# A second expert layer with its table stationary: sums that come out with model dimensions on partitions

## The chip, the cores and the metric

One core of a Trainium2 chip runs the whole program. The metric is the device time of one execution in microseconds. Of the core's engines, TensorE (PE) multiplies matrices, with a stationary operand that is loaded ahead and a moving one of up to 512 columns that streams past it; VectorE (DVE) and ScalarE (ACT) do elementwise work; SyncE (SP) issues transfers.

## The reference

Two blocks over 256 tokens of 1024 model dimensions. Each ends with an expert layer (`peer`) of 16384 experts of one neuron each, 8 heads, 16 chosen per head; the second block's layer does the same with its own weights and shared keys. The rest of both blocks (attention and recurrences, cross attention) stands ahead of these layers.

```python
def peer(xn, w_pq, subkeys, peer_u, peer_v):
    ...                                # scores, top 16 of each half, top 16 of the sums
    gate = jax.nn.softmax(best_s, axis=-1).astype(xn.dtype)
    ...
        act = jax.nn.gelu(jnp.einsum('thkd,td->thk', peer_u[eb], xb), approximate=False) * gb
        return jnp.einsum('thk,thkd->td', act, peer_v[eb])
...
        x = x + peer(rmsnorm(x, g_peer[l]), w_pq[l], peer_subkeys[l], peer_u[l], peer_v[l])
    return rmsnorm(x, g_final)
```

The second block takes the first one's normalized x, begins with a norm of its own, and its result is normalized with `final_g_2`.

## The kernel before

x lies transposed: eight blocks `X[k]` of 128 model dimensions on partitions, 256 tokens along them. An expert layer is computed densely: all 16384 experts are applied to all tokens, with gates that are zero where an expert was not chosen. The 16384 experts are 128 tables of 128 experts; a table of the first layer (`u`) and one of the second (`v`) have 128 x 1024 numbers.

Every table comes by DMA as `raw` (four buffers) and is split by `weight` (L282 to L290) in two halves of 512 columns, each into a high part `wh` (ACT, L274) and the rest `wl` (DVE, L275), seven buffers a half of each. A product is three matmuls: high by high, high by rest, rest by high (L298 for the first layer, tile `ph`: per table 24 matmuls, eight blocks of the table stationary, 256 tokens moving).

The gated activations come from `prep` (L1210): `hid` is multiplied with the gates `gt` (DVE, L1218), which `fetch` (L1208) has SP load from `gd` in memory, and is split into `dah` (ACT, L274) and `dal` (DVE, L275), four tables in one call. The loop at the end of `peer` takes the 128 `v` tables in order; for each it issues the matmuls of the second layer (L1274), then the next piece of a `u` table as long as there are any (`ug`; `AHEAD` is 47, so that 94 of the 128 `u` tables are done ahead of the loop and the other 34 lie between the first `v` tables), then the next step of `prep` for the four tables behind. With the `u` tables gone, `v` tables follow each other, and `prep` runs as far ahead of them as buffers let it.

The second layer has the activations stationary (128 tokens a time) and the table moving, 512 columns: 12 matmuls for a table, into four PSUM banks `acc[th][dh]`, tokens on partitions (`th` a half of the tokens, `dh` of the dimensions). The last two tables are taken bank by bank, so that banks are complete one after another. `tokens` (L1252) adds x by 16 matmuls with the identity, in the second half of the loop.

Between the peers, `between` (L1286) copies the four banks to `xt`, transposes them by 16 matmuls (`pot`, L1306), copies the result into x (L1310, L1312), feeds the next norm's split input `xnh` (ACT, L408) and `xnl` (DVE, L411), on which the next projections `mm` start, and makes the statistics of both norms from `xt`: four Squares 1024 wide with sums along the free side (L1318, L1321), a product with `gfin` (L1319), an rsqrt by small DVE steps, and `spread` (L371), which brings the factors to the layout of x. At the end `finish` (L1341) reads the banks directly: four Squares, products with `gfin` (L1351), the rsqrt, the scaling and the store.

The order of each engine's instructions is that of the code, with the streams interleaved by a scheduler at build time; each engine runs its own in that order and waits at semaphores.

Of the kernel before, what the change touches and what calls it, by code (L numbers as in the profile page):

```python
# [233 lines left out]
class Net:  # L234
# [679 lines left out]
    def patterns(self):  # L914

        nc = self.nc
        self.iota2 = self.sm("iota2", 256, F16).rearrange("p (i t) -> p i t", t=2)
        nc.vector.tensor_copy(self.iota2, self.c("iota").unsqueeze(2).broadcast_to([128, 128, 2]))
        self.iota16, self.runs16 = (self.sm(n, 256, BF16).rearrange("p (a r) -> p a r", a=16)
                                    for n in ("iota16", "runs16"))  # L920
        for y, x in ((self.iota16, self.c("iota", 16)), (self.runs16, self.c("runs"))):
            nc.vector.tensor_copy(y, x.unsqueeze(2).broadcast_to([128, 16, 16]))
# [68 lines left out]
    def peer(self, N, g, wpq, sub, shared, u, v, gelu, final):  # L991

# [251 lines left out]
        acc = [[self.ac("acc") for _ in range(2)] for _ in range(2)]  # L1244
        gf = None

        def tokens():

            nc.sync.dma_start(gf, final)
            for th in range(2):  # L1250
                for k in range(8):
                    nc.tensor.matmul(acc[th][k // 4][:, k % 4 * 128:k % 4 * 128 + 128],  # L1252
                                     self.X[k][:, 128 * th:128 * th + 128], self.c("ident"), start=False, stop=False)
                    if k % 4 == 3:
                        yield

        xg = tokens()
        for i0 in range(0, 128, 4):
            pn = prep(i0 + 4) if i0 < 124 else iter(())
            ah, al = ops[i0]  # L1260
            w = {}
            for i in range(4):
                w[i] = self.weight(v[i0 + i])

                todo = [(i, q % 2, q // 2) for q in range(4)]
                if i0 + i == 126:
                    todo = []
                elif i0 + i == 127:
                    todo = [(2 + q % 2, q // 4, q // 2 % 2) for q in range(8)]
                for n, th, dh in todo:  # L1270
                    wh, wl = w[n]
                    sl = slice(th * 128, th * 128 + 128)
                    for j, (l, r) in enumerate(((ah, wh), (ah, wl), (al, wh))):
# [5 lines left out]
                if i0 >= 64:  # L1279
                    if gf is None:  # L1280
                        gf = self.big("gfin")
                    next(xg, None)
            drain(pn)
        return acc, gf

    def between(self, acc, gf):  # L1286
# [3 lines left out]
        gg = self.sm("gg", 8)  # L1290
        tt(gg, self.s("g_final"), self.s("norm1_g_2"), ALU.mult)
        xt = []
        for th in range(2):
            xt.append(self.big(f"xt{th}"))
            for dh in range(2):
                sl = slice(512 * dh, 512 * dh + 512)
                if dh:
                    nc.scalar.activation(xt[th][:, sl], acc[th][dh], AF.Copy)
                else:
                    nc.vector.tensor_copy(xt[th][:, sl], acc[th][dh])  # L1300
        for cp in range(4):
            pt = self.mm("pot")
            for a in range(2):
                for th in range(2):
                    c = cp * 2 + a
                    nc.tensor.transpose(pt[:, a * 256 + th * 128:a * 256 + th * 128 + 128],  # L1306
                                        xt[th][:, c * 128:c * 128 + 128], self.c("ident"))
            d = self.x[:, 2 * cp:2 * cp + 2, :].rearrange("p a t -> p (a t)")
            if cp % 2:
                nc.vector.tensor_copy(d, pt)  # L1310
            else:
                nc.scalar.activation(d, pt, AF.Copy)  # L1312
        N = self.norm(self.X, gg, "xn", stats=False)

        v, r = self.sm("bv4", 4), self.sm("br4", 4)
        for th in range(2):
            y = self.big("bty")
            nc.scalar.activation(y, xt[th], AF.Square, accum_out=v[:, th:th + 1])  # L1318
            tt(xt[th], xt[th], gf, ALU.mult)  # L1319
            y = self.big("bty")  # L1320
            nc.scalar.activation(y, xt[th], AF.Square, accum_out=v[:, 2 + th:3 + th])  # L1321
        ts(v, v, 1.0 / D, None, ALU.mult)
# [18 lines left out]
    def finish(self, acc, gf):  # L1341
        nc = self.nc
        tt, ts = nc.vector.tensor_tensor, nc.vector.tensor_scalar
        for th in range(2):
# [166 lines left out]
    def run(self):  # L1511
        tc, nc, I = self.tc, self.nc, self.I
        from contextlib import ExitStack
        with ExitStack() as es:
# [18 lines left out]
            final = [I["gfin"][i:i + 1, :].broadcast_to([128, 1024]) for i in range(2)]  # L1533
            N = self.between(*self.peer(N, self.s("g_peer"), I["w_pq"], I["sub1"], False, I["u1"], I["v1"], AF.Gelu,
                                        final[0]))
            N = self.mixer2(N)
            self.finish(*self.peer(N, self.s("norm2_g_2"), I["w2_pq"], I["sub2"], True, I["u2"], I["v2"],
                                   AF.Gelu_apprx_tanh, final[1]))
# [38 lines left out]
```

## Time and profile before

| | us |
|---|---|
| median of 3 runs (2197.25 to 2197.65) | 2197.36 |
| the profiled execution | 2197.23 |
| its span | 2195.4 |
| PE busy | 2173.8 (99%) |
| weight loads on PE, beside its matmuls | 1979.0 (90%) |
| DVE busy | 1627.1 (74%) |
| ACT busy | 1217.0 (55%) |
| DMA, mean over the span | 201 GB/s |

The span runs from the first instruction to the last; 1.8 us of the execution lie outside it. A matmul's duration in a row includes its way through the array, so neighbours overlap; the distance of two starts is what one costs in a row of them. A chain of waits is read from the last instruction back, at each step to what released it.

### The profile page before, as it was taken

Reading aid. Unit: us, or ns where it says so; the run is one execution under the profiler, and the core shown is the slowest. Engines: PE = TensorE matmul, PEld = TensorE weight load, DVE = VectorE, ACT = ScalarE, POOL = GpSimd, SP = SyncE. Lnnn points to the kernel's source line nnn. Section 1 sums busy time; section 2 is a strip of 40 time slices with the busy share of each in tenths; the row PEclk is TensorE's granted clock in tenths of the full one; section 3 lists DMA queues with packets and bytes.
Section 4 is the critical chain, followed back from the end, with each engine's and each line's share of the span. In section 5 each row is a group of like instructions: output and inputs, shape, how many; then the busy total and the mean of one; then the engine's idle time right before and its main releaser. Section 6 shows DMA issues by size and latency. Waiting matters only on the chain.

```text
span 2195.4 us, 40524 instructions
## 1 busy us (share of the span) xinstructions
PE 2173.8 (99%) x15268; PEld 1979.0 (90%) x15268; DVE 1627.1 (74%) x3504; ACT 1217.0 (55%) x2237; POOL 1.8 (0%) x12
## 2 busy tenths in 40 slices
PE   8999999999999999999999999999999999999998
PEld 8899799999999999888887799999999999887886
DVE  8786676999998665687446567898999655688544
ACT  6463455655666555655445545655666655565443
POOL 0000000000000000000000000000000000000000
PEclk9999999999999999999999999999999999999999
DMA  6442355465677776797555445556577866687653
GB/s 230 141 154 89 118 159 173 146 204 181 212 277 263 238 226 207 236 293 247 186 188 185 147 129 185 161 183 196 196 262 266 262 208 212 220 289 243 214 188 125
DMA packets 178679, 441.12 MB, mean 201 GB/s; under 512 B 13602, under 2 KB 79266, under 8 KB 178484
## 3 DMA queue, kind: packets, MB, share of 16 engines
q1 hardware_dynamic: 177764, 437.11, 61.2%
q8 instruction: 119, 1.95, 0.4%
q10 hardware_dynamic: 720, 1.44, 0.2%
q14 instruction: 76, 0.62, 0.1%
HBM read 403.89 MB, written 34.60 MB: 200 GB/s over the span
## 4 chain that ended last, share of the span: by engine, by line
PE 93%; DVE 4%; DMA 1%; ACT 1%; issue 1%; SPq 0%; ACTq 0%; DVEq 0%
PE ph L298 33%; PE acc L1274 30%; PE mm L298 18%; PE mm L339 3%; PE pg L1164 3%; DVE wl L275 1%; DMA gt<-gd 1%; PE psc L1027 1%; DVE dal L275 0%; PE px L665 0%; ACT wh L274 0%; PE pp L673 0%; DVE hid L1218 0%; PE cs L937 0%; PE pt L679 0%
## 5 line engine op out<-in xcount | busy, mean ns | idle before, releaser
L274 ACT ACTIVATE wh<-raw 128x512 fp32r<-128x512 f32 x1388 | 864.4, 630 | 820.5 <-PE ph L298 272.8
L275 DVE TENSOR_TENSOR wl<-raw,wh 128x512 fp32r<-128x512 f32 x1388 | 941.8, 687 | 437.3 <-ACT wh L274 433.1
L298 PE MATMUL ph<-pxh,wh 128*128 128x256 f32 x2048 | 578.8, 283 | 0.0
L298 PE MATMUL ph<-pxh,wl 128*128 128x256 f32 x2048 | 572.1, 279 | 0.0
L298 PE MATMUL ph<-pxl,wh 128*128 128x256 f32 x2048 | 571.2, 279 | 0.0
L1274 PE MATMUL acc<-wl,dah 128*128 128x512 f32 x1024 | 405.6, 396 | 0.9 <-DVE wl L275 0.4
L1274 PE MATMUL acc<-wh,dah 128*128 128x512 f32 x1024 | 405.5, 396 | 0.0
L1274 PE MATMUL acc<-wh,dal 128*128 128x512 f32 x1024 | 405.0, 396 | 0.0
L298 PEld LDWEIGHTS ph<-pxl,wh 128*128 128x128 f32 x2048 | 385.1, 188 | 3.2
L298 PEld LDWEIGHTS ph<-pxh,wh 128*128 128x128 f32 x2048 | 385.0, 188 | 3.1
L298 PEld LDWEIGHTS ph<-pxh,wl 128*128 128x128 f32 x2048 | 384.8, 188 | 0.0
L1274 PEld LDWEIGHTS acc<-wl,dah 128*128 128x128 f32 x1024 | 192.4, 188 | 46.0 <-DVE wl L275 3.4
L1274 PEld LDWEIGHTS acc<-wh,dal 128*128 128x128 f32 x1024 | 192.4, 188 | 46.0
L1274 PEld LDWEIGHTS acc<-wh,dah 128*128 128x128 f32 x1024 | 192.4, 188 | 43.2
L298 PE MATMUL mm<-xnh,wh 128*128 128x256 f32 x496 | 143.6, 289 | 8.9 <-ACT wh L274 8.1
L298 PE MATMUL mm<-xnh,wl 128*128 128x256 f32 x496 | 141.8, 286 | 0.0
L298 PE MATMUL mm<-xnl,wh 128*128 128x256 f32 x496 | 141.3, 285 | 0.0
L274 ACT ACTIVATE dah<-hid 128x512 fp32r<-128x512 f32 x128 | 76.3, 621 | 81.8 <-DVE hid L1218 80.8
L1218 DVE TENSOR_TENSOR hid<-hid,gt 128x512 f32<-128x512 f32 x128 | 85.7, 686 | 45.1 <-DMA gt<-gd 44.9
L298 PEld LDWEIGHTS mm<-xnh,wh 128*128 128x128 f32 x496 | 95.8, 193 | 11.2 <-ACT wh L274 8.1
L298 PEld LDWEIGHTS mm<-xnh,wl 128*128 128x128 f32 x496 | 95.5, 193 | 0.9 <-issue 0.6
L298 PEld LDWEIGHTS mm<-xnl,wh 128*128 128x128 f32 x496 | 95.8, 193 | 0.5 <-issue 0.3
(446 smaller groups left out, 2849.2 us busy)
## 6 DMA issues: line engine op xcount, KB each, us to landing
raw<-in_u_dram SPq DMA_DIRECT2D x256, 512.0 KB, 4.0
raw<-in_v_dram SPq DMA_DIRECT2D x256, 512.0 KB, 4.3
gd<-S SPq DMA_DIRECT2D x64, 512.0 KB, 4.8
gt<-gd SPq DMA_DIRECT2D x64, 512.0 KB, 5.7
raw<-in_w_gate_dram SPq DMA_DIRECT2D x32, 512.0 KB, 3.6
raw<-in_w_pq_dram SPq DMA_DIRECT2D x32, 512.0 KB, 3.7
raw<-in_w_g_dram SPq DMA_DIRECT2D x12, 512.0 KB, 4.7
raw<-in_w_qk_dram SPq DMA_DIRECT2D x8, 512.0 KB, 3.7
```

What stands on the lines that cost most here:

```text
L274: self.nc.scalar.activation(hi, src, AF.Copy)
L275: self.nc.vector.tensor_tensor(lo, src, hi.bitcast(F32), ALU.subtract)
L298: self.nc.tensor.matmul(out, l, r, start=i == 0, stop=i == n - 1)
L339: nc.tensor.matmul(ps[th], l, r, start=k == 0 and j == 0, stop=k == 7 and j == 2)
L1027: nc.tensor.matmul(pz[:, p * 128:p * 128 + 128], qf[:, p * 256 + th * 128:p * 256 + th * 128 + 128], key(h, p), start=True, stop=True)
L1164: nc.tensor.matmul(pg[:, t * 128:t * 128 + 128], part[c][:, b, :, e], hot[:, b, 0, :, e], start=c == 0, stop=c == 1)
L1218: tt(hv, hv, gv, ALU.mult)
L1274: nc.tensor.matmul(acc[th][dh], l[:, n, sl], r.half[dh], start=i0 + n == 0 and j == 0, stop=i0 + n == 127 and j == 2)
```

## The change

The second layer's operands change places. A block of a table (128 experts by 128 dimensions) is stationary and the activations of all 256 tokens stream: 24 matmuls of 256 columns for a table where 12 of 512 stood. The banks hold model dimensions on partitions, two blocks of x in each. Four matmuls of 16-bit zeros open them in each peer. The x matmuls of `tokens` are gone: as each pair of blocks is complete, `sum_up` adds the bank to x (DVE, L1288 of the changed kernel). The last two tables go block by block. `between` has no copies and transposes; its statistics are four Squares of x, 512 wide (L1304), whose sums over dimensions come from 16 full-precision matmuls `ss` with four moving columns (L1308), one weight for each of the two norms. `finish` transposes x by 16 matmuls (`ot`, L1338) and goes on as before. The product with `gfin` stands in the second peer alone.

```diff
-        acc = [[self.ac("acc") for _ in range(2)] for _ in range(2)]
+        acc = [self.ac("acc") for _ in range(4)]
+        for a in acc:
+            nc.tensor.matmul(a, self.zero16, self.wide16, start=True, stop=False)
...
-        def tokens():
-            nc.sync.dma_start(gf, final)
-            for th in range(2):
-                for k in range(8):
-                    nc.tensor.matmul(acc[th][k // 4][:, k % 4 * 128:k % 4 * 128 + 128],
-                                     self.X[k][:, 128 * th:128 * th + 128], self.c("ident"), start=False, stop=False)
...
+        def second(n, blocks, w):
+            ah, al = ops[n // 4 * 4]
+            wh, wl = w
+            for d in blocks:
+                o = acc[d // 2][:, d % 2 * 256:d % 2 * 256 + 256]
+                for j, (l, r) in enumerate(((wh, ah), (wh, al), (wl, ah))):
+                    nc.tensor.matmul(o, l[d], r[:, n % 4, :], start=False, stop=n == 127 and j == 2 and d % 2 == 1)
...
-                        nc.tensor.matmul(acc[th][dh], l[:, n, sl], r.half[dh], start=i0 + n == 0 and j == 0,
-                                         stop=i0 + n == 127 and j == 2)
+                if n < 126:
+                    second(n, range(8), w[n])
+                elif n == 127:
+                    for d in range(8):
+                        second(126, (d,), w[126])
+                        second(127, (d,), w[127])
+                        if d % 2:
+                            self.sum_up(acc[d // 2], d // 2)
...
+    def sum_up(self, acc, b):
+        x = self.x[:, 2 * b:2 * b + 2, :].rearrange("p a t -> p (a t)")
+        self.nc.vector.tensor_tensor(x, x, acc, ALU.add)
...
+        ss = self.ac("ss")
+        for b in range(4):
+            sq = self.big("bty", (2, 256))
+            nc.scalar.activation(sq, self.x[:, 2 * b:2 * b + 2, :], AF.Square)
+            for a in range(2):
+                for th in range(2):
+                    k = 2 * b + a
+                    nc.tensor.matmul(ss[:, 0:4], sq[:, a, 128 * th:128 * th + 128],
+                                     wt[:, k, 2 - 2 * th:6 - 2 * th], start=k == 0 and th == 0,
+                                     stop=k == 7 and th == 1)
...
+        acc = [[self.mm("ot") for _ in range(2)] for _ in range(2)]
+        for k in range(8):
+            for th in range(2):
+                nc.tensor.transpose(acc[th][k // 4][:, k % 4 * 128:k % 4 * 128 + 128],
+                                    self.X[k][:, 128 * th:128 * th + 128], self.c("ident"))
```

Elsewhere each engine's order is as it was; the first and second layers alternate as before. It differs at three places.

DVE at the end of the first peer's preparation, and between the peers; `wl` rows up to the count are second-layer halves and the first halves of the weights behind. Before:

```order
L275 TENSOR_TENSOR wl<-raw,wh 128x512
L275 TENSOR_TENSOR dal<-hid,dah 128x512 x2
L275 TENSOR_TENSOR wl<-raw,wh 128x512 x116
L1300 COPY xt_13934<-acc 128x512
```

Now:

```order
L275 TENSOR_TENSOR wl<-raw,wh 128x512 x120
L1288 TENSOR_TENSOR x<-x,acc 128x512
L411 SCALAR_TENSOR_TENSOR xnl_15469<-x,gg,xnh_15468 128x256
L1288 TENSOR_TENSOR x<-x,acc 128x512
L411 SCALAR_TENSOR_TENSOR xnl_15469<-x,gg,xnh_15468 128x256
```

Behind the last `dal` stand four more halves (120 for 116, of which three belong to the next weights in either), and the sums into x with the next input's parts take the place of the copies. In the second peer the count is 113 in both.

ACT between the peers; `wh` are second-layer halves and then those of the next projections. Before:

```order
L1298 ACTIVATE xt_13937<-acc 128x512
L1312 ACTIVATE x<-pot 128x512
L274 ACTIVATE wh<-raw 128x512
L1312 ACTIVATE x<-pot 128x512
L408 ACTIVATE xnh_13964<-x,gg 128x256 x4
L408 ACTIVATE xnh_13966<-x,gg 128x256 x4
```

Now:

```order
L274 ACTIVATE wh<-raw 128x512 x121
L408 ACTIVATE xnh_15468<-x,gg 128x256 x2
L274 ACTIVATE wh<-raw 128x512 x2
L408 ACTIVATE xnh_15468<-x,gg 128x256 x2
L274 ACTIVATE wh<-raw 128x512
L408 ACTIVATE xnh_15470<-x,gg 128x256 x4
L1304 ACTIVATE bty<-x 128x512 x4
L274 ACTIVATE wh<-raw 128x512 x8
```

The copies are gone, `wh` halves stand between the parts of `xnh`, and the four Squares come in a row behind the last of them.

PE in the projections behind that place, now (before, no row stands between the `mm` rows there):

```order
L298 MATMUL mm<-xnh_15470,wl 128x256
L1308 MATMUL ss<-sqw,bty 128x4 x4
L298 MATMUL mm<-xnh_15470,wh 128x256
L298 MATMUL mm<-xnl_15471,wh 128x256
L298 MATMUL mm<-xnh_15470,wl 128x256
L298 MATMUL mm<-xnh_15470,wh 128x256
L1308 MATMUL ss<-sqw,bty 128x4 x4
```

The `ss` matmuls come in fours, each four behind one Square, and PE takes the projection rows behind them only after.

## Rows read from the trace of the kernel before

**Rows 1.** The page: busy time by engine; the chain by line, shares of the span.

```profile
PE 2173.8 (99%) x15268; PEld 1979.0 (90%) x15268; DVE 1627.1 (74%) x3504; ACT 1217.0 (55%) x2237; POOL 1.8 (0%) x12
...
PE ph L298 33%; PE acc L1274 30%; PE mm L298 18%; PE mm L339 3%; PE pg L1164 3%; DVE wl L275 1%; DMA gt<-gd 1%; PE psc L1027 1%; DVE dal L275 0%; PE px L665 0%; ACT wh L274 0%; PE pp L673 0%; DVE hid L1218 0%; PE cs L937 0%; PE pt L679 0%
```

**Rows 2.** The chain of waits, first peer: start us, us, engine, tile, line, count.

```profile
428.01 70.01 PE ph L298 x600
...
607.40 2.88 PE ph L298 x24
...
725.49 2.79 PE acc L1274 x12
728.27 2.80 PE ph L298 x24
```

**Rows 3.** The chain, where the x matmuls stand in the first peer.

```profile
1002.68 0.89 PE acc L1252 x8
```

**Rows 4.** Busy time by engine, PEclk, DMA share, GB/s; DVE's stretches of both peers.

```profile
908.20:1021.20 113.00, 113.00 (x523) 92.66 (x523) 101.00 (x166) 69.36 (x126) 0.00 (x0) 1.00 0.88 282
1910.40:2028.50 118.10, 117.31 (x538) 94.74 (x536) 101.12 (x166) 68.04 (x125) 0.00 (x0) 1.00 0.85 270
```

**Rows 5.** DVE's groups in the first peer's stretch: busy, mean ns, idle before.

```profile
L275 DVE TENSOR_TENSOR wl<-raw,wh 128x512 fp32r<-128x512 f32 x76 | 51.0, 684 | 0.7 <-ACT wh L274 0.7
...
L1218 DVE TENSOR_TENSOR hid<-hid,gt 128x512 f32<-128x512 f32 x44 | 29.5, 686 | 12.0 <-DMA gt<-gd 12.0
```

**Rows 6.** The same view in the second peer's stretch.

```profile
L1218 DVE TENSOR_TENSOR hid<-hid,gt 128x512 f32<-128x512 f32 x44 | 29.6, 686 | 17.0 <-DMA gt<-gd 16.8
```

**Rows 7.** DVE's timeline at both stretches' ends: start us, us, what.

```profile
1019.78 1.28 DVE L275 TENSOR_TENSOR dal<-hid,dah 128x512 fp32r<-128x512 f32 x2
...
2027.05 1.28 DVE L275 TENSOR_TENSOR dal<-hid,dah 128x512 fp32r<-128x512 f32 x2
```

**Rows 8.** The chain at the end of the second peer's stretch.

```profile
2028.99 11.22 PE acc L1274 x47
```

**Rows 9.** Timeline between the peers: start us, us, what, idle before and its releaser.

```profile
1182.44 1.97 PE L1306 MATMUL pot<-const,xt 128*128 128x128 f32 x16
...
1184.63 3.30 ACT L408 ACTIVATE xnh<-x,gg 128x256 fp32r<-128x256 f32 x8
...
1185.18 0.39 PE L298 MATMUL mm<-xnh,wh 128*128 128x256 f32 x1 [0.78 <-ACT xnh L408]
...
1200.25 0.40 PE L339 MATMUL mm<-wl,xnh 128*128 128x512 f32 x1
...
1200.76 1.13 PE L371 MATMUL spread<-dg,const 128*128 128x256 f32 x4
```

**Rows 10.** The chain at the gate matmuls of the second peer.

```profile
1712.61 0.93 PE pg L1164 x16
```

**Rows 11.** PE's timeline at full-precision matmuls with few columns.

```profile
65.41 0.37 PE L581 MATMUL gc<-g,const 128*128 128x8 f32 x2
65.64 1.14 PE L431 MATMUL l<-const,l2sq 128*128 128x128 f32 x8
```

**Rows 12.** Timeline of the tail.

```profile
2185.78 0.20 DVE L1352 TENSOR_SCALAR fv<-fv 128x1 f32<-128x1 f32 x1
...
2186.82 0.40 PE L1274 MATMUL acc<-wh,dal 128*128 128x512 f32 x1
...
2187.25 0.60 ACT L1350 ACTIVATE bty<-acc 128x512 f32<-128x512 f32 x1 [0.71 <-PE acc L1274]
...
2191.13 0.72 ACT L1360 ACTIVATE fino<-fino,fr 128x512 f32<-128x512 f32 x1 [1.39 <-DVE fr L359]
```

**Rows 13.** Granted clock after a thin stretch, and the chain there.

```profile
1300.00:1310.00 10.00, 10.00 (x57) 9.64 (x58) 3.14 (x5) 2.39 (x4) 0.00 (x0) 0.66 0.16 53
...
1300.32 0.72 PE pm L1474 x2
1301.04 15.03 PE mm L298 x103
```

More of the change, by code (lines that the diff above doesn't have):

```diff
@@ L1261, in peer @@
             w = {}
[L1262 to L1273, printed above, removed]
-                        nc.tensor.matmul(acc[th][dh], l[:, n, sl], r.half[dh], start=i0 + n == 0 and j == 0,
-                                         stop=i0 + n == 127 and j == 2)
+            for n in range(i0, i0 + 4):
+                w[n] = self.weight(v[n])
+                if n < 126:
[6 more added lines that the diff above has]
+                            self.sum_up(acc[d // 2], d // 2)
@@ L1277, in peer @@
                 next(ug, None)
                 next(pn, None)
[L1279 to L1282, printed above, removed]
+                if i0 >= 64 and final is not None and gf is None:
+                    gf = self.big("gfin")
+                    nc.sync.dma_start(gf, final)
             drain(pn)
-        return acc, gf
-    def between(self, acc, gf):
+        return gf
+    def sum_up(self, acc, b):
+        x = self.x[:, 2 * b:2 * b + 2, :].rearrange("p a t -> p (a t)")
+        self.nc.vector.tensor_tensor(x, x, acc, ALU.add)
@@ L1288, in between @@
+    def between(self):
         nc = self.nc
         tt, ts = nc.vector.tensor_tensor, nc.vector.tensor_scalar
-        gg = self.sm("gg", 8)
+        gg, wt = self.sm("gg", 8), self.sm("sqw", 48).rearrange("p (k n) -> p k n", n=6)
         tt(gg, self.s("g_final"), self.s("norm1_g_2"), ALU.mult)
[L1292 to L1300, printed above, removed]
@@ L1301, in between @@
-        for cp in range(4):
-            pt = self.mm("pot")
+        nc.vector.memset(wt, 0.0)
+        nc.vector.memset(wt[:, :, 2], 1.0)
+        tt(wt[:, :, 3], self.s("g_final"), self.s("g_final"), ALU.mult)
+        N = self.norm(self.X, gg, "xn", stats=False)
+        ss = self.ac("ss")
+        for b in range(4):
+            sq = self.big("bty", (2, 256))
+            nc.scalar.activation(sq, self.x[:, 2 * b:2 * b + 2, :], AF.Square)
             for a in range(2):
                 for th in range(2):
[L1305 to L1312, printed above, removed]
@@ L1339, in between, with finish @@
         return N
-    def finish(self, acc, gf):
+    def finish(self, gf):
         nc = self.nc
         tt, ts = nc.vector.tensor_tensor, nc.vector.tensor_scalar
+        acc = [[self.mm("ot") for _ in range(2)] for _ in range(2)]
[3 more added lines that the diff above has]
+                                    self.X[k][:, 128 * th:128 * th + 128], self.c("ident"))
         for th in range(2):
@@ L1532, in run @@
             N = self.cross(N, kv)
[L1533 to L1538, printed above, removed]
+            self.peer(N, self.s("g_peer"), I["w_pq"], I["sub1"], False, I["u1"], I["v1"], AF.Gelu, None)
+            N = self.mixer2(self.between())
+            self.finish(self.peer(N, self.s("norm2_g_2"), I["w2_pq"], I["sub2"], True, I["u2"], I["v2"],
+                                  AF.Gelu_apprx_tanh, I["gfin"][1:2, :].broadcast_to([128, 1024])))
 class Rows:
```

16 lines of the change are left out of this document (4 added, 12 removed).

## The prediction

> **What bounds the kernel now.** I began with the page: TensorE (PE) is busy in 99% of the span and the chain that ended last runs over it for 93%, a third in first-layer matmuls (`ph`) and 30% in second-layer ones (`acc`) [rows 1]. So what counts is PE's time, and the few places where PE waits. The profiled execution took 2197.23 us, 1.83 more than its span; the median of the three shown is 2197.36, so both may stand for each other, and the sums below are made against 2197.2. About 0.2% (4.4 us) is what a measurement of this kernel can tell from no change.
>
> The chain gives the price of a table in either layer where nothing waits: 12 matmuls of 512 columns in 2.79 to 2.80 us, 24 of 256 columns in 2.80, and 600 of 256 in 70.01, 116.7 ns each [rows 2]. The 16 matmuls that add x into the sums are on the chain too, eight records in 0.89 four times over in a peer: 3.56 us [rows 3].
>
> Then I looked for where PE waits. In the long stretch after the last first-layer table, VectorE (DVE) must prepare two things: weight halves (`wl`) and the gated activations (`hid`, `dal`). The 113.0 us of it in the first peer and the 118.1 of the second hold 166 DVE operations each [rows 4]; in the first, `hid` waits 12.0 us for gates `gt` to come [rows 5]; the second waits 17.0 for them [rows 6]. The last `dal` ends at 1021.06 and at 2028.33 [rows 7]. In the first peer PE has a lead of tables and never stops; in the second the lead runs out, and PE goes on unhindered only from 2028.99 [rows 8]. From the stretch's start to the end of the last second-layer matmul it is 1182.44 - 908.2 = 274.2 us in the first, and 2187.05 - 1910.4 = 276.7 in the second [rows 4, 9, 12]: the same matmuls, 2.4 us of waits.
>
> **The change part by part.** *The turned matmuls.* 128 tables a peer go from 12 x 512 to 24 x 256 columns. By the rows, 0: a table of 24 is at 2.80 and one of 12 at 2.80 [rows 2]. The worst row for 24 is 2.88, right behind the gate matmuls; it would make 256 x 0.08 = 20.5 us, but a single table is at 2.80 between two second-layer tables, which is the place at issue, so I take 0. The Trainium skill states a fixed price of some 2.5 ns for each matmul at the full clock (TensorE: Matmul & The Clock Gate, "Wait — 56ns, not 53.3ns?"); by the page, 2 x 128 x 12 more matmuls would be an estimated 7.7 us and the sum 2213.5, and these rows do not show it.
>
> *The zero matmuls* that open the banks: four a peer, 512 columns, 16-bit. Sixteen f16 matmuls of 128 columns take 0.93 [rows 10], 58 ns, so 512 columns 0.23; eight of them +1.9 us, on PE's path in both peers, ahead of DVE's stretch, whose start they shift. Filling the zeros is DVE work at the very start, 0 since it lies hundreds of microseconds ahead of its user and DVE is idle a quarter of the run [rows 1]; were that cover gone, two fills at under 0.7 each.
>
> *The x matmuls go,* 3.56 us a peer, and here I part from the easy answer of -7.1. PE gets nothing from them if it only reaches the end of DVE's preparation earlier. After the last `dal` the order has 113 halves left in both peers before, and 117 and 113 after; at 1.40 us of PE for a half (2.80 for two) that is 158.2 and 163.8. Second peer before: 2028.33 + 158.2 = 2186.5, 0.5 short of its measured end, which is the step from a half to its matmuls: DVE sets this end. First peer before: 1021.06 + 158.2 + 0.5 = 1179.8, against 1182.44, so PE has 2.7 of lead to give and no more. After, in the first peer: the stretch has four halves less, left for later (112.9 - 4 x 0.60 = 110.5; two such operations in a row take 1.28 and one 0.68, so each further one is 0.60 [rows 5, 7]), and PE ends at 908.2 + 110.5 + 163.8 + 0.5 = 1183.0, that is +0.6; with the second peer's waits for gates it is +5.6; never less than PE alone, -3.6. In the second peer after, the same 75 halves stand in the stretch, so a stretch of 117.9 gives 0 and one of 112.9 gives -5.0; PE alone -6.0. The two peers do the same work with waits of 12.0 and 17.0 for gates, and I can't see from the trace which comes: the middle, -2.5. Both peers together -1.9, between -9.6 and +5.6.
>
> *Between the peers.* Gone are the copies, 16 transposes and their copies back: from the last second-layer matmul to the next matmul 1182.44 to 1185.18, 2.74 us, and 0.28 at `spread`, which starts at 1200.76 where the matmul ahead ended at 1200.48 [rows 9]: 3.0 in all. In their place DVE adds each pair of blocks to x (0.69, as a `wl` or `hid`, of 512 columns too [rows 5]), ScalarE (ACT) and DVE make `xnh` and `xnl` of it (0.41 each [rows 9]). In the order, ACT has the next table's `wh` in its queue ahead of `xnh` of the later blocks, so PE waits: 0.69 for the last sum, then 0.6 for `wh`, as long as a Square [rows 12], and 0.41 for `xnh`, with issue gaps 1.74. Then 16 `ss` matmuls in full precision, with x squared as the stationary side and four columns moving, between the `mm` rows, on PE's path. The nearest rows are two-record matmuls with eight columns whose successor starts 0.23 later [rows 11]: 16 x 0.23 = 3.7. Their Squares are four ACT operations of 0.60 behind the eight `xnh`; PE runs in order, so a `ss` that waits for a Square holds the projections behind it, and the rsqrt on DVE, which starts after the last `ss`, holds `spread`: some 1.2. Sum 6.7 for 3.0, +3.7. If the waits all hide behind `mm` work, 3.7 - 3.0 = +0.7; if each is as long as a Square and a `wh` together (1.2) for three of the four groups, +5.5.
>
> *The tail.* Before, three of the four Squares read finished banks while PE still ran; only one follows the last matmul, which ends at 2186.82 + 0.23 = 2187.05, and the last scaling starts at 2191.13 [rows 12], 4.08 us later. After, the last sum (0.69) must end before the last four of 16 transposes; the 16 take 1.97 [rows 9]; the banks of token half 0 are complete only with the last block, so its second Square (0.60 [rows 12]) and the read of its sum end about 3.4 behind the last matmul. DVE's row of small steps from its first `fv` to the last scaling is 2191.13 - 2185.78 = 5.35 long and without a gap [rows 12]. 3.5 + 5.35 = 8.9 for 4.08: +4.9; +3.5 if the transposes overlap the last sums, +5.5 with a further Square in the way.
>
> Sum: 1.9 - 1.9 + 3.7 + 4.9 = +8.6, 2205.8 us.
>
> **The rivals.** *The gates come in time (not slower).* If the DMA of `gt` is early enough that DVE's stretch falls by its 12 to 17 us of waits, the tokens' time is gained in full, and the second peer's waits too: -9.6 in place of -1.9, total +0.9, 2198.1. For it: the first peer shows 5 us less of waits at the same work. Against: 0.88 and 0.85 of the DMA share is taken there [rows 4], and the change asks for no byte less in that stretch. It decides in full from a DVE stretch under 106.4 us in the first peer (110.5 less the 0.6 and 3.6) and 112.0 in the second (117.9 less 6.0), 4 to 6 us of waits less. 0.17.
>
> *The statistics hide.* The `ss` matmuls cost a fraction, as their moving side has four columns only, and PE's waits stay under those of before: between -1.5 and 0 in place of +3.7, 2200.6 at -1.5, which I take for it (before's 3.0 halved). For it: 15 us of `mm` matmuls lie there, from 1185.18 to 1200.48 [rows 9], to fill holes. Against: PE's order is fixed, so a row that waits holds all behind it. 0.11. Both rivals at once: 2200.6 - 7.7 = 2192.9, faster; 0.03.
>
> *PE's clock falls in the thin stretch* after the last second-layer table, where PE has transposes, waits and four-column matmuls. The trace has such a place: after small full-precision matmuls (`pm`) the granted clock was 0.66 over the next 10 us [rows 13], between its levels 1.2 and 2.4 GHz, and 103 matmuls that take 12.0 at 116.7 ns took 15.03: +3.0. 2208.8; 0.05. Against it: the stretch here has long `mm` matmuls between the thin ones.
>
> *The price of a matmul.* If a matmul has a price of its own that only shows where the stationary side changes with streamed activations, the worst row of 24 holds: +20.5 on top, 2226.3. 0.02; for it only the 2.88 rows, against it 600 matmuls in 70.01 with a new stationary block each.
>
> **How the numbers follow.** The forecast has 0.62, with its own range 2202 to 2211: the ends of between (+0.7 to +5.5) and of the tail (+3.5 to +5.5) and the second peer's 0 to -5.0, added as independent ones (2.4, 1.0 and 2.5 to a side: 3.6, and 1 for what I left at nothing). Of the rest 0.17 + 0.11 + 0.03 lie below it and 0.07 above. The range that leaves out 2 in 10 takes in most of the first rival: 2197.5 to 2212. Within 0.2% is 2193.0 to 2201.8: the first two rivals, 0.27 with rounding. Faster 0.04, the pair of rivals with a little more; slower 0.69. The change does what it says by its order; that the matmuls are twice as many is not in doubt.
>
> **What would show it.** In the profile after: `acc` groups of 256 columns with a mean near that of `ph`; a table at 2.80 in the chain, as in [rows 2]; DVE's stretch near 110 and 113 to 118 with idle time on `gt`; the end of the first peer's last `acc` near 1184 (0.5 and the zeros' 0.9 later than 1182.44); 6 to 7 us from there to steady `mm`, counting `ss`; and 8 to 9 us from the last `acc` to the last scaling. I am wrong if a table takes 2.88 or more, if DVE's stretch falls under 107 in the first peer, or if the `ss` rows start much closer than 0.2 us apart.

## The result

The changed kernel takes 2228.18 us (median of 4 runs, 2220.89 to 2232.98) against 2197.51 for the kernel before: a ratio of 1.0135, with a 95% interval of 1.0106 to 1.0163. It is slower, as forecast, but by 30.7 us and not by 8.6, and outside the range (2197.5 to 2212). The profiled execution is the fastest of the four, 2220.89, so its 23.7 us over the profiled execution of the kernel before are what this trace can explain.

The page of the changed kernel, busy time by engine and the two second-layer and first-layer groups with the most time (columns as in [rows 1]; the groups give operands, count, busy us and mean ns):

```profile
PE 2195.3 (99%) x18316; PEld 2139.5 (96%) x18316; DVE 1629.6 (73%) x3511; ACT 1212.3 (55%) x2229; POOL 1.9 (0%) x12
...
L298 PE MATMUL ph<-pxh,wh 128*128 128x256 f32 x2048 | 581.8, 284 | 0.0
L1260 PE MATMUL acc<-dah,wl 128*128 128x256 f32 x2048 | 576.9, 282 | 2.2 <-DVE wl L275 1.7
```

PE is busy in 99% of the span as before, so nothing on the page says what went wrong. The chain of waits does, in two places:

```profile
429.72 71.00 PE ph L298 x600
...
729.82 0.88 PE acc L1250 x4
730.70 2.84 PE acc L1260 x24
733.53 2.84 PE ph L298 x24
736.37 2.84 PE acc L1260 x24
```

The 600 first-layer matmuls, which the change does not touch and which run 300 us ahead of its first matmul, took 71.00 us where [rows 2] have 70.01: 118.3 ns each in place of 116.7. A table of 24 takes 2.84 where 2.80 was, in either layer. The granted clock in both traces is 1.00 there.

From the timelines of four traces, the span cut at the first `ph` matmul, the ends of the last second-layer matmuls (`acc`) and the last scaling, in us. A matmul's end is taken 0.12 behind its start at 256 columns and 0.23 at 512, where the next one of a row would start. a576 and a576p are experiments below:

| stage | before | after | a576 | a576p |
|---|---|---|---|---|
| start to first `ph` | 427.77 | 429.48 | 428.50 | 428.04 |
| first peer, to its last `acc` | 754.67 | 764.67 | 757.92 | 752.03 |
| to the second peer's first `ph` | 247.57 | 249.52 | 248.32 | 252.60 |
| second peer, to its last `acc` | 757.04 | 763.01 | 758.99 | 752.05 |
| last `acc` to last scaling | 4.08 | 8.05 | 8.05 | 8.06 |
| behind it | 4.32 | 4.36 | 4.37 | 4.37 |

The new parts of the change can be read in the trace of after. Between the peers and at the end its chain has these rows:

```profile
1194.31 1.18 PE mm L298 x10
...
1196.78 0.95 PE ss L1308 x8
...
1201.04 0.79 PE ss L1308 x8
...
1208.78 1.10 PE spread L371 x4
```

The first `mm` follows the last `acc` matmul at once: in the timeline it starts at 1194.15, 0.12 behind the start of that one (the chain counts from its modelled end). The four groups of `ss` take 3.32 in all, and `spread` is 14.6 us behind the last `acc`, where [rows 9] have 18.3; 20 fewer `mm` matmuls of 512 columns stand ahead of it (33, where there were 53).

```profile
2206.84 1.65 PE ot L1338 x15
...
2209.93 0.12 DVE fv L1348
...
2214.73 0.72 ACT fino L1356
```

On this chain DVE's `fv` is 3.25 us behind the last `acc` matmul, the last scaling 8.05.

### The profile page after: what moved, and what is told of

Its sections match the earlier page's. It is cut to its first block, busy times and chain, and to the rows that moved or that the text cites. A ratio compares the mean times of both kernels' runs of the same rounds, so it can differ in the third digit from the quotient of the medians.

```text
span 2219.1 us, 46863 instructions
## 1 busy us (share of the span) xinstructions
PE 2195.3 (99%) x18316; PEld 2139.5 (96%) x18316; DVE 1629.6 (73%) x3511; ACT 1212.3 (55%) x2229; POOL 1.9 (0%) x12
## 4 chain that ended last, share of the span: by engine, by line
PE 93%; DVE 3%; DMA 2%; ACT 1%; issue 1%; SPq 0%; ACTq 0%; DVEq 0%
PE ph L298 33%; PE acc L1260 30%; PE mm L298 17%; PE mm L339 3%; PE pg L1166 3%; DVE wl L275 1%; DMA gt<-gd 1%; PE psc L1029 1%; DMA raw<-in_v_dram 0%; PE px L665 0%; PE pp L673 0%; ACT wh L274 0%; PE cs L940 0%; PE pt L679 0%; DVE dal L275 0%
## 5 line engine op out<-in xcount | busy, mean ns | idle before, releaser
L1260 PE MATMUL acc<-dah,wl 128*128 128x256 f32 x2048 | 576.9, 282 | 2.2 <-DVE wl L275 1.7
L1260 PE MATMUL acc<-dah,wh 128*128 128x256 f32 x2048 | 575.7, 281 | 0.0
L1260 PE MATMUL acc<-dal,wh 128*128 128x256 f32 x2048 | 575.3, 281 | 0.0
L1260 PEld LDWEIGHTS acc<-dah,wl 128*128 128x128 f32 x2048 | 385.9, 188 | 4.5 <-DVE wl L275 4.0
L1260 PEld LDWEIGHTS acc<-dah,wh 128*128 128x128 f32 x2048 | 385.9, 188 | 0.2
L1260 PEld LDWEIGHTS acc<-dal,wh 128*128 128x128 f32 x2048 | 385.9, 188 | 0.1
```

Source lines behind the costliest of these rows:

```text
L1260: nc.tensor.matmul(o, l[d], r[:, n % 4, :], start=False, stop=n == 127 and j == 2 and d % 2 == 1)
```

## The experiments

**Where the matmul's price comes from.** The candidates were a state of the execution or the chip (S), the change's own matmuls (C), and placement (P). The change takes three small tiles, `zero16`, `wide16` and `sqw`, of 256 + 1024 + 192 bytes in each partition, from the pool of small tiles. The pool behind it holds the activations, one operand of nearly every matmul. By the addresses in the built programs it begins at byte 89440 before and at 90912 after; the pool of weights, which holds the other operand, stays at 28480. So the distance of the two operands' pools goes from 60960 to 62432, from 32 to 224 modulo 256. Four kernels moved the pool, and the few small tiles that lie between the unused one and it, and nothing else. The unused tile is set to zero once at the very start:

```diff
         nc.vector.tensor_copy(self.iota2, self.c("iota").unsqueeze(2).broadcast_to([128, 128, 2]))
+        self.pad = self.sm("pad", 144)
+        nc.vector.memset(self.pad, 0.0)
```

with 144 numbers for a576, 368 for b1472, 8 for a32 and b32 (a: the changed kernel, b: the kernel before; the digits are bytes).

> The changed kernel with 576 unused bytes more in the pool of small tiles, so that the pool behind it (activations, inputs of every matmul) begins at 91488, which is 2048 bytes from where it began before the change (89440); the change itself had pushed it by 1472. Theory P (placement): a matmul of 256 columns costs 116.7 or 118.3 ns by where in a partition its operands lie; expects long rows of ph and acc at 116.7 ns as before and the time down by 14000 x 1.66 ns = 23 us or more, to 2195 to 2206, with runs that agree within 3 us. Theory S (a state of the execution or of the chip): nothing to do with addresses; expects 118.3 ns and 2220 to 2233 as for the changed kernel. Theory C (the change's own matmuls are dear): ph at 118.3 as it is in the changed kernel, 2220 to 2233.

Measured: 2208.46 (2206.00 to 2209.67), ratio 1.0050 [1.0033, 1.0066]. The chain of a576, first-layer rows and the second layer's first tables:

```profile
428.74 70.00 PE ph L298 x600
...
726.21 0.88 PE acc L1252 x4
727.09 2.80 PE acc L1262 x24
729.89 2.80 PE ph L298 x24
```

Unused bytes took 16 to 20 us off the change, and a turned table is at 2.80. S and C fall. The time is still 2.5 us above the range that P gave; the part on the x matmuls below looks for the rest.

> The kernel before with 1472 unused bytes in the pool of small tiles: the pool behind begins at 90912, as in the changed kernel, and nothing else differs. Theory P: ph rows at 118.3 ns, second-layer matmuls of 512 columns unchanged at 233.3; 6144 ph and some 1700 mm of 256 columns x 1.66 = +13 us, 2208 to 2214, perhaps with runs that spread. Theories S and C: 2197.4 as the kernel before.

Measured: 2206.40 (2205.93 to 2210.91), ratio 1.0048 [1.0031, 1.0064]. The kernel before, with nothing added but space, pays the same price for its first layer, from the chain of b1472:

```profile
430.26 71.00 PE ph L298 x600
```

Its 512-column matmuls stay at 233.3 ns apart. The time is 1.6 us below P's range: in places the kernel before is not at 116.7 ns but at 117.6 on average, and has less to lose there.

> The changed kernel with 32 unused bytes: the pool begins at 90944, a multiple of 64 (64 modulo 128, as the pool of weights). Theory P leaves open which rule of place counts: if it is a start at a multiple of 64, 116.7 ns or less and 2195 to 2206; if it is the place modulo 128 or 1024 as before, no gain, 2220 to 2233. Theories S and C: 2220 to 2233.

Measured: 2247.87 (2243.06 to 2253.55), 1.0239 [1.0222, 1.0256]: dearer still, above every guess. From the chain of a32:

```profile
432.14 71.99 PE ph L298 x600
```

120.0 ns a matmul; a start at a multiple of 64 is not the rule, and here both pools lie at 64 modulo 256.

> The kernel before with 32 unused bytes: the pool begins at 89472, a multiple of 128. Theory P: if the start at a multiple of 64 counts, 116.7 ns throughout, also where the kernel before had 117.8 in some stretches (2000 matmuls x 1.1 = -2 us), 2193 to 2198; if the place as it was before is the only good one, 2205 to 2214. Theories S and C: 2197.4.

Measured: 2202.00 (2200.25 to 2205.15), 1.0022 [1.0013, 1.0032], 600 `ph` in 70.67, 117.8 ns. Both guesses missed: neither the best price nor that of b1472.

**Place or distance.** Two kernels told apart whether the activations' own place counts. b128 has 128 unused bytes; bk32 has 32 ahead of the pool of weights, so that both pools move:

```diff
             self.x = keep.tile([128, 8, 256], F32, name="x")
+            self.pad = keep.tile([128, 8], F32, name="padk")
+            nc.vector.memset(self.pad, 0.0)
```

> The kernel before with 32 unused bytes ahead of the pool of weights, so that weights and activations both move by 32 (weights from 64 to 96 modulo 128, activations from 96 to 0). If the distance of the two pools counts, it is kept: 116.7 ns and 2195 to 2199. If the activations' own place counts: 117.8 ns as with the pool of activations alone at 0 modulo 128, 2200 to 2205.

Measured: 2196.41 (2194.15 to 2200.76), 0.9999 [0.9990, 1.0008]; 600 `ph` in 70.01, and also the slower stretches of the kernel before (117.6 on average between 600 and 700 us) come back in the same places. With the activations alone moved by 32 (b32) it was 70.67. In this one shift it is the distance that counts. The pool of weights holds `raw` too, and the other pool more than the activations, so that it is the two reads of a matmul that meet is the simplest reading, and not shown.

> The kernel before with 128 unused bytes: the pool of activations begins at 89568, the same modulo 128 as at 89440 but another modulo 256, 512 and 1024. If the place modulo 128 sets the price of a matmul: long ph rows at 116.7 ns, 2195 to 2199 as before. If it is a place in larger steps: another spacing, 2200 or more, or less than 2190.

Measured: 2209.28 (2206.07 to 2211.09), 1.0060 [1.0045, 1.0076], 600 `ph` in 70.41 in the first peer and in 71.21 (118.7 ns) in the second, and 120.0 ns in other rows: the place modulo 128 does not set the price.

**The changed kernel again,** for a second trace.

> The changed kernel as it is, for a second trace of it and its times beside the others on one chip. Theory P expects 118.3 ns for 256 columns again, in first-layer and second-layer rows alike, and 2220 to 2233; the difference from run to run should then lie in the waits of the second peer's preparation and not in the spacing.

Measured: 2224.63 (2220.52 to 2228.66), 1.0121 [1.0106, 1.0137]; its profiled execution took 2228.66. 118.3 ns again, in all long rows. The two traces are 7.8 us apart, 1.2 of it ahead of the first `ph`, 2.8 and 2.1 in the peers and 1.6 between them; the guess put it into the second peer's waits alone. In the peers the stretch of preparation is longer: the last `dal` of the first ends 106.1 us behind the last `ph` in place of 103.3, of the second 109.6 in place of 107.5, with 13.6 and 15.1 us of waits for gates in place of 10.2 and 12.7. Between the peers PE's granted clock fell to 0.50, 1.2 GHz, within the last `ss` rows; after had 1.00 there. The same 29 `mm` matmuls in the chains of after and then a_again, and a_again's window (columns as in [rows 4]):

```profile
1201.83 6.88 PE mm L339 x29
...
1206.05 8.27 PE mm L339 x29
...
1205.60:1209.00 3.40, 3.40 (x10) 2.77 (x10) 2.88 (x10) 0.63 (x1) 0.00 (x0) 0.50 0.16 25
```

**The x matmuls.** a576 leaves 11 us over the kernel before, and its first peer is 3.3 slower although 3.56 us of x matmuls are gone. b_notok takes these matmuls out of the kernel before and changes nothing else in the code:

```diff
                 for k in range(8):
-                    nc.tensor.matmul(acc[th][k // 4][:, k % 4 * 128:k % 4 * 128 + 128],
-                                     self.X[k][:, 128 * th:128 * th + 128], self.c("ident"), start=False, stop=False)
                     if k % 4 == 3:
```

> The kernel before without the 16 matmuls of each peer that add x into the sums (x is left out of both sums, nothing takes its place); places in memory are unchanged. Theory D (DVE's preparation sets both ends, so PE's 3.56 us a peer are not gained in full): by the steps of the prediction, the first peer gains at most its lead of 2.7 and the second 0 to 2.5; 2192 to 2197, likeliest 2194.5. Theory G (the tokens' time is gained in full): 7.1 to 9.5 less, 2187 to 2190.

Measured: 2187.40 (2186.62 to 2190.88), 0.9963 [0.9950, 0.9977]: 9.1 less, theory G in size. In its trace the first peer is 3.53 shorter and the second 5.90, the x matmuls and the 2.4 of waits. But the order that the scheduler made is another one here: behind the last `dal` DVE has 113 and 109 halves left instead of 117 and 113 (counted in the traces up to the last `acc`, so with four of the next weights in the first peer), so preparation is spread over more tables. D's arithmetic with these counts, 2022.1 + 109 x 1.40 + 0.5 = 2175.2, lies below PE's end, 2176.4. So G's number doesn't refute D's mechanism. In a576 the order went the other way: 121 and 113. The windows of a576 and b_notok in the stretch (columns as in [rows 4]):

```profile
917.20:1021.50 104.30, 101.79 (x846) 99.35 (x845) 92.69 (x152) 61.66 (x114) 0.00 (x0) 1.00 0.83 270
...
1923.40:2033.10 109.70, 107.62 (x896) 105.18 (x896) 94.21 (x155) 62.25 (x115) 0.00 (x0) 1.00 0.84 271
```

```profile
917.20:1021.50 104.30, 104.30 (x448) 83.97 (x447) 94.92 (x156) 66.77 (x118) 0.00 (x0) 1.00 0.91 289
```

The first of these two blocks is a576's two peers, the second b_notok's first. 846 matmuls at 116.7 ns are 98.7 us of the 104.3, so PE stopped for 5.6 us, and for 5.2 in the second (896: 104.5 of 109.7). The busy column shows less than half of it, as a matmul's modelled end hides the first part of each gap: the count is the better reading. b_notok's 448 of 512 columns are 104.5 of 104.3: none. PE's waits in a576's first stretch name DVE (us in total, times, longest):

```profile
PE acc L1262 <- DVE wl L275: 1.9, 4, 0.9
```

**Even preparation.** a576p keeps each step of preparing activations behind the last `wl` that stands ahead of it in the code (an ordering on DVE alone):

```diff
-                tt(hv, hv, gv, ALU.mult)
+                x = tt(hv, hv, gv, ALU.mult)
+                if i0 > 0:
+                    self.after(x.ins, self.lastwl.ins)
                 yield
...
-                self.split(ah[:, i:i + 2, :], al[:, i:i + 2, :], h[:, i:i + 2, :])
+                x = self.split(ah[:, i:i + 2, :], al[:, i:i + 2, :], h[:, i:i + 2, :])
+                if i0 > 0:
+                    self.after(x.ins, self.lastwl.ins)
```

with `lastwl` set in `weight`.

> a576 (the change at the good distance), with each step of preparing the gated activations kept behind the last weight half that was written ahead of it in the code, so that DVE takes one such step per table instead of two to three. Theory D (in a576 the dense preparation starves PE of weight halves, 5.8 us of stops in the first peer's stretch and 5.5 in the second's, and that is where the time of the x matmuls went): stops near 0, 11 us less than a576, 2195 to 2199. If the stops come from something else (transfers of the tables, say): as a576, 2205 to 2210.

Measured: 2196.03 (2194.62 to 2199.12), 0.9999 [0.9989, 1.0009]. DVE's groups in a576p's first stretch, and its window:

```profile
L275 DVE TENSOR_TENSOR wl<-raw,wh 128x512 fp32r<-128x512 f32 x75 | 52.0, 693 | 31.5 <-ACT wh L274 28.8
L1222 DVE TENSOR_TENSOR hid<-hid,gt 128x512 f32<-128x512 f32 x20 | 13.7, 685 | 0.0
L275 DVE TENSOR_TENSOR dal<-hid,dah 128x512 fp32r<-128x512 f32 x18 | 12.3, 684 | 0.0
```

```profile
916.80:1021.20 104.40, 104.40 (x898) 104.40 (x897) 73.48 (x113) 58.12 (x96) 0.00 (x0) 1.00 0.74 238
```

DVE now has 38 steps of preparation in 104 us where [rows 4, 5] have 90 in 113 (166 operations, 76 of them `wl`); it waits for gates nowhere, and PE runs through: 898 matmuls, 104.8 us of work. The first peer is 5.9 us shorter than in a576, the second 6.9. Theory D holds. At this place and in this order the change costs 1.2 us over the kernel before in the same order (bp, below), no more than the noise.

> The kernel before with the same even preparation. Theory D: its 2.6 us of stops in the second peer's stretch vanish, and no more, as the first peer has none: 2193 to 2195. If even preparation makes weights late elsewhere: 2196 or more.

Measured: 2194.86 (2194.00 to 2195.57), 0.9993 [0.9984, 1.0003]; the second peer is 2.4 us shorter in the trace. The trace agrees with D, the times alone can't tell it from no change.

> The changed kernel at its own placement (distance 224 modulo 256), with the even preparation of a576p and nothing else. If the two causes add: 118.3 ns for 256 columns, no stops in the stretches, and the 12 us that even preparation took off at the other distance, 2211 to 2218 (14500 matmuls x 1.66 = 24 over a576p at most, less what the kernel before pays in its own slower stretches). If slower matmuls already hid the stops: 2220 or more.

Measured: 2218.89 (2217.92 to 2221.00), 1.0110 [1.0093, 1.0127]. The time lies between the two guesses. By the ratios (1.0121 and 1.0135 before) even preparation takes 2.4 to 5.5 us off at the change's own distance, less than the 11 at the better one. In the traces its two peers together are 5.4 us shorter than those of after and 10.3 shorter than those of a_again, against 12.8 from a576 to a576p, while the stretch between the peers is 3.2 and 1.6 longer, with the clock down again. By the count of matmuls PE stopped for 3.3 and 1.6 us in after's two stretches and for 6.0 and 3.7 in a_again's, against 5.6 and 5.2 in a576. So slower matmuls may hide some of the stops, but one execution differs from the next by as much. The runs agree within 3 us, where those of after spread over 12; that the spread was in the waits for gates fits and is not shown.

**The tail.** a576pt is a576p with the transposes of each pair of blocks set one pair later between the last tables, by a function `turn` that is called in the loop.

```diff
...
+                        if d in (3, 5, 7) and final is not None:
+                            self.turn(d - 3, d - 1)
+                    if final is not None:
+                        self.turn(6, 8)
...
```

> a576p, and the 16 transposes of the end placed behind each pair of blocks of the last two tables, so that only four follow the last sum. Theory T (the tail's 4 us over the kernel before are the transposes and Squares behind the last matmul): 1.5 to 2.5 us less than a576p from the last second-layer matmul to the last scaling, 2193 to 2197. If DVE's chain of small steps alone sets it: no difference to a576p.

Measured: 2199.34 (2196.49 to 2199.81), 1.0009 [0.9999, 1.0018]. Theory T falls. In its chain two groups of transposes stand between the last `acc` rows, so these end 0.9 us later, and from the last of them to the last scaling only 0.3 is saved:

```profile
2179.08 0.44 PE ot L1300 x4
2179.52 1.40 PE acc L1266 x12
2180.92 0.44 PE ot L1300 x4
...
2185.55 0.12 DVE fv L1362
...
2190.36 0.72 ACT fino L1370
```

From `fv` to the last scaling it is 4.81 in a576pt and 4.80 in after, and from the second peer's first `ph` to the last scaling 760.67 against 760.11 in a576p. DVE's chain behind the two Squares sets the tail. The median of a576pt is 3.3 us above that of a576p, more than the traces differ. The granted clocks of its runs go with it: three runs at 2196.5 to 2197.1 have a mean of 0.996, the seven at 2198.5 to 2199.8 have 0.994 or 0.995, and a difference of 0.0015 of such a run is an estimated 3 us. Only one of the low ones was profiled, so where the clock was down in the others no trace shows.

**All distances.** Four kernels with even preparation took further distances; a288pt is a576pt at 256 modulo 512, ap128, ap160 and ap224 are the changed kernel with even preparation and so many unused bytes.

> a576pt with 288 unused bytes in place of 576: the pool of activations lies at a distance of 62720 from the pool of weights, 256 modulo 512. So far the distance modulo 512 was 0 (120.0 ns for 256 columns), 32 (116.7), 64 (117.8), 160 (117.4 and more) and 480 (118.3). Theory P says that this distance has a spacing of its own, the same in all long rows of 256 columns; it does not say which. At 116.7 it would be as a576pt; every ns more or less is 14 us in 14000 matmuls.

Measured: 2242.14, 1.0203 [1.0186, 1.0220], 600 `ph` in 71.99, as a32.

> The changed kernel with even preparation and 128 unused bytes: distance 62560, 96 modulo 256. If the price goes by how far the distance is from a multiple of 64 or 256: 116.7 to 118.3 and 2196 to 2218. A new lowest spacing, under 116.5 ns, would give under 2193.

Measured: 2243.84, 1.0221 [1.0204, 1.0238], 72.00: no help.

> The same with 160 unused bytes: distance 62592, 128 modulo 256, a multiple of 64 as the 117.8 of distance 64. If the distance modulo 64 counts: 117.8 ns, 2206 to 2212; if only modulo 256: any other.

Measured: 2227.96, 1.0152 [1.0135, 1.0169], 72.00, and 118.7 ns in other stretches. The distance modulo 64 does not set the price.

> The same with 224 unused bytes: distance 62656, 192 modulo 256, the mirror of 64. If the price is the same on both sides of a multiple of 256: 117.8 ns, 2206 to 2212; distances 32 and 224 (116.7 and 118.3) speak against that, and then 118 to 120 and 2212 to 2242.

Measured: 2191.39 (2186.31 to 2196.74), 0.9974 [0.9964, 0.9985]: faster than the kernel before, against the guess of 2206 or more. The trace has two spacings, 113.4 and 117.8 ns, in different rows.

Two last kernels asked whether this is the distance modulo 256, and whose gain it is.

> ap224 with 480 unused bytes in place of 224: distance 62912, 192 modulo 256 as before, 448 in place of 192 modulo 512. If the distance modulo 256 is all that counts: long rows at 114.3 or 117.8 ns and 2186 to 2197. If a larger step counts: another spacing, at 118.3 or more 2205 to 2245.

Measured: 2191.99 (2187.51 to 2197.84), 0.9981 [0.9971, 0.9991]. From its chain:

```profile
423.37 68.02 PE ph L298 x600
...
716.94 2.83 PE acc L1266 x24
719.77 2.83 PE ph L298 x24
```

113.4 ns in the first 600 matmuls, 117.8 where the layers alternate and in the whole second layer. The distance does not tell which of the two holds: the same 600 matmuls of ap480's second peer are at 117.8, and so are those of ap224 in both peers. A row keeps its spacing until other matmuls come between. In the first peer three `pid` matmuls stand between two long rows of `ph`, and there the spacing changes, one way in ap480 (113.4 to 117.8) and the other way in ap224. The first three lines are from ap480's chain, the last three from ap224's:

```profile
496.94 30.72 PE ph L298 x271
527.99 39.58 PE ph L298 x336
...
1420.44 70.67 PE ph L298 x600
...
426.57 70.67 PE ph L298 x600
...
498.13 36.75 PE ph L298 x312
535.21 38.10 PE ph L298 x336
```

> bp (the kernel before with even preparation) with 160 unused bytes: distance 61120, 192 modulo 256. If the place alone is the gain: its 256-column rows at 114.3 or 117.8 ns, 512-column rows at 229 to 233.3, 2175 to 2196. If the gain needs the turned matmuls: 512-column rows at 233.3 and the 256-column ones no cheaper than 116.7 on the whole, 2195 to 2203.

Measured: 2164.63 (2161.25 to 2167.87), 0.9857 [0.9843, 0.9871], faster than the 2175 at which the guess began. It beats both kernels. From its chain:

```profile
423.39 68.02 PE ph L298 x600
...
716.09 2.75 PE acc L1280 x12
718.83 2.75 PE ph L298 x24
721.58 2.75 PE acc L1280 x12
```

A table of 12 matmuls of 512 columns takes 2.75, 229.0 ns a matmul, and the `ph` between them 114.4. The place is the gain, and the change as made costs here: 2.83 for 2.75 in 256 second-layer tables, 20 of the 27 us between ap480 and bp160, and as much for each of the `ph` tables between them, 68 in both peers, 5 us.

All distances together, from the spacing of neighbouring matmuls in unbroken rows of the traces. The distance is that of the activations' pool from the weights' pool; with 256 columns the weights are stationary, with 512 the activations:

| distance modulo 256 | kernels | 256 columns, ns | 512 columns, ns |
|---|---|---|---|
| 0 | a32, a288pt | 120.0 | 226.7 to 228.1 |
| 32 | before, bk32, b_notok, a576, a576p, a576pt, bp | 116.7 and 117.8 | 233.3 |
| 64 | b32 | 117.8, in a few rows 113.3 | 233.3 |
| 96 | ap128 | 120.0 | 234.3 |
| 128 | ap160 | 118.7 and 120.0 | 232.4 to 233.4 |
| 160 | b128 | 117.3, 118.7 and 120.0 | 233.3 to 234.1 |
| 192 | ap224, ap480, bp160 | 113.3 and 117.8 | 228.9 to 229.5 |
| 224 | after, a_again, b1472, ap | 118.3 | 233.3 |

Kernels of one row show the same spacings, and in the rows of 0 and 192 their distances differ modulo 512. Where there are two or three, which one holds in a stretch is not set by the distance.

## Why the prediction was wrong, point by point

**The step that failed first is "Filling the zeros is DVE work at the very start, 0".** It costed the instructions that fill the new tiles, and nothing was set down for their 1472 bytes. These moved every activation against every weight, from 32 to 224 modulo 256, and PE pays 1.66 ns for each of some 14000 matmuls of 256 columns, the untouched ones too: 23 us. a576 gives back 16 to 20 us of the 30.7 (2228.18 and 2224.63 to 2208.46) with unused bytes; against the trace of after it loses some of the 23 again to longer stops of PE. It stands at 2208.46, inside the range. That it does is in part luck, as the terms below missed in both directions. None of the rivals had it: the trace of before can't show a place that the kernel didn't have.

**The turned matmuls at 0** were right at the old distance (2.80 in a576, and 2.80 in [rows 2]), and only there. At 224 a turned table takes 2.84 where 12 of 512 still take 2.80 (b1472's stay at 233.3 ns): of the price of placement, 256 x 0.04 = 10 us belong to turning. At 192 it is 2.83 to 2.75. That 24 matmuls of 256 columns cost what 12 of 512 do held for one placement.

The Trainium skill's 2.5 ns for each matmul (TensorE: Matmul & The Clock Gate, "Wait — 56ns, not 53.3ns?") isn't what shows: at a distance of 32 the difference between two matmuls of 256 and one of 512 is 0 ns, at 0 it is 12 to 13, at 192 it is -2 or 6, so no fixed price fits.

**The x matmuls, -1.9** came as +3.4 in a576 (first peer 757.92 - 754.67, second 758.99 - 757.04, less 0.9 of zeros each), inside the term's -9.6 to +5.6. The reason given was the right one: DVE's dense preparation sets both ends, and PE gets nothing from fewer matmuls. The step's own sum, with a576's ends of the last `dal`, gives 1021.50 + 163.8 + 0.5 = 1185.8 and 2033.08 + 158.2 + 0.5 = 2191.8, where PE ended at 1186.42 and 2193.73; about 1.5 of the second difference is a spacing of 117.8 from 2030 on. The size was off because DVE's stretch did not become shorter as was taken: counted from the last 44 `hid`, it took 108.6 us and not 109.5 in the first peer and 114.8 for 114.6 in the second, with 12.0 and 15.8 us of waits for gates. Seen from PE this is its stops of 5.6 and 5.2 us. With even preparation the terms are what PE alone would give: 752.03 - 0.9 - 754.67 = -3.5 and -5.9.

**The zeros, +1.9**: 0.88 a peer in the chain, +1.8. Right.

**Between the peers, +3.7**: +0.75 in a576. Of its parts `ss` was 3.3 for 3.7; the wait of 1.74 at the start was 0 and the 1.2 at `spread` didn't come. The blocks of x are complete one after another while PE is still at the last tables, so the first `mm` found its input there: the step let the chain begin with the last sum. This is the low end of the term, +0.7, with all waits hidden, and not the rival that the statistics hide, as the `ss` matmuls cost nearly what was taken for them. (The term's upper end comes out of the waits that it names as +6.0 and not +5.5.)

**The tail, +4.9**: +3.97 (8.05 for 4.08). The steps were right. From its first `fv`, DVE's row of small steps takes 4.89 (4.80 on the chain) where 5.35 was taken over. The two Squares of a token half lie 0.57 us apart in place of 1.40, which fits; no run separates it.

**The clock rival,** at 0.05, exists. In the trace of after the granted clock is 1.00 throughout between the peers, but in a_again, the same kernel, it fell there. In all, it fell to 0.50 behind the first `ss` rows, for a few us, in 7 of the 12 traces of kernels with the table stationary (a_again, ap, ap128, ap160, a288pt, a576p, a576pt), and in none of the 8 of kernels without (before, bk32, b32, b128, b1472, b_notok, bp, bp160). In six of the seven the 29 `mm` matmuls behind the `ss` rows took 8.1 to 9.6 us, where after has 6.88. The longest is a576p's, with 0.77 over the 15 us from 1185:

```profile
1186.98 1.20 PE ss L1314 x8
1188.17 9.59 PE mm L339 x29
```

That is most of the 4.3 us by which a576p's stage is longer than a576's, and a_again's stage is 1.6 longer than after's: the price that was set, +3.0, lies between. It comes with the change in some executions and not in others: some of the difference between the median of after, 2228.18, and its profiled 2220.89 may be this.

## What to carry to other kernels

A price per instruction that is read from a trace holds for the addresses that this program had: where a change adds or drops a tile, compare where the pools behind it begin, and try a few unused bytes before the change itself is judged, as the place can cost more than the change. Where PE is busy in 99%, count its matmuls in a window and multiply with the spacing; the busy share hid both the slower spacing and over half of the stops. And a step taken off PE is worth its time only as long as the order of the engine that feeds it leaves PE a lead, which an even order gave here for nothing (bp, 0.9993).

## What was not expected of the hardware

The spacing of matmuls with a newly loaded stationary block of 128 x 128 and 32-bit operands goes with the distance between the two operands' pools in a partition, modulo 256 bytes: 113.3 to 120.0 ns for 256 columns and 226.7 to 234.3 for 512, at a granted clock of 1.00, 2.4 GHz. It isn't how either operand is aligned, as far as one shift of both can show (bk32). Distances of 32 and 224 differ, and so do 64 and 192 at 512 columns (233.3 and 229), so it isn't symmetric. At some distances the spacing has more than one value. A long row keeps the one that it begins with (117.8 over 3897 matmuls in ap480, where the layers alternate and behind), and it changes where other matmuls or a stop come between, not always the same way. In the kernel before 117.8 stands at the same places in both peers; at 192, in ap480 and bp160, the peers differ. What chooses the value, and the reason for the whole effect, are open. Distances that aren't multiples of 32 were not tried.
